# Hybrid encoder trunk on one core: places and order of the rotary queries and weight halves in the attention heads

## The chip, the core and the metric

The kernel runs on one core of one Trainium2 chip. Its engines work side by side, each through its own list of instructions in order: TensorE (PE, with its weight loads PEld) multiplies and transposes, VectorE (DVE), ScalarE (ACT) and GpSimd (POOL) work element by element, and SyncE (SP) starts the transfers from HBM to SBUF. Matmuls write to PSUM, from where DVE and ACT read.

The metric is the device time of one execution in microseconds (us). A change is judged by the median of several runs.

## The reference

The model has two layers over 256 tokens of width 2048, all in float32. Layer 0 mixes tokens with a convolution module, layer 1 with multi-head latent attention (16 heads), and each is followed by a squared-ReLU MLP of width 8192. The change is in the attention:

```python
down = h @ w_in
c_q, c_kv, k_pe = jnp.split(down, [Q_LORA_RANK, Q_LORA_RANK + KV_LORA_RANK], axis=-1)
q = (rms_norm(c_q, q_norm_g) @ w_q_up).reshape(B, S, N_HEADS, QK_NOPE_DIM + QK_ROPE_DIM)
q_nope, q_pe = jnp.split(q, [QK_NOPE_DIM], axis=-1)
q_pe = apply_rope(q_pe, cos[:, :, None, :], sin[:, :, None, :])
k_pe = apply_rope(k_pe, cos, sin)
kv = (rms_norm(c_kv, kv_norm_g) @ w_kv_up).reshape(B, S, N_HEADS, QK_NOPE_DIM + V_HEAD_DIM)
k_nope, v = jnp.split(kv, [QK_NOPE_DIM], axis=-1)
...
s = (jnp.einsum('bqhd,bkhd->bhqk', qn, k_nope)
     + jnp.einsum('bqhr,bkr->bhqk', qp, k_pe)).astype(jnp.float32) * scale
...
p = jax.nn.softmax(s, axis=-1).astype(v.dtype)
return jnp.einsum('bhqk,bkhd->bqhd', p, v)
```

Here `S` is 256, a head has 128 plain and 64 rotary query columns and 128 value columns, and a mask lets a token see only its own and earlier chunks of 64.

## The kernel before

**Numbers in two parts.** A float32 operand of a matmul is split into a high part (ACT copies it to a narrower type, `hi`) and a low part (DVE subtracts, `lo`); three matmuls make one product (`mm3`, L178). Weights come as units of 0.5 or 1 MB in a `raw` tile (three places) and are split in two halves (`split_half`, L148): one copy on ACT (L154) and one subtraction on DVE (L155) each, 128 x 1024 for most units, 128 x 512 for the rotary query units, into six places for halves.

**Pieces.** The attention part is one list in an order written out by hand (`manual_schedule`, L1147), and each engine gets its instructions in that order. The 16 heads form four groups of four (`HG`, `NG`). What a group needs ahead of its heads is cut into pieces:
- `qn_piece` (L1005): the plain queries of one head, transposed: 12 matmuls, then ACT writes `qTh` and DVE `qTl`;
- `qp_piece` (L1020): the rotary queries of four heads for one block `t` of 128 tokens: 12 matmuls, ACT copies PSUM to `qr` (L1030), POOL turns it in six steps (`rope`, L837 to L842) into `qp`, then ACT and POOL split `qp` into `qhl` (`qp_parts`, L1046);
- `kv_piece` (L978): keys of one head (`c` 0 or 1: `kTh`, `kTl`) or values of two heads for one block of tokens (`c` 2 or 3: DVE copies to `vv`), 12 matmuls each.

A group has four plain query pieces, two rotary ones and eight key and value pieces. While the heads of group g run, the pieces of group g+1 are put between their steps (during the last group, pieces of the output product).

**Steps of a head.** `scores(h)` (L1083): ten matmuls into one PSUM tile, then DVE takes the maxima (L1098, L1099) and ACT the exponentials (L1101). `weights(h)` (L1106): DVE scales (L1108, L1111). `weights_turn(h-1)` (L1113): three transposes on PE and a copy on ACT. `qp_turn` (L1050): four transposes of `qhl` for two heads of the next group, and two copies on ACT (`qpA` L1064, `qpB` L1065); the scores of these heads read `qpA` and `qpB` (L1095, L1096). `values(h-2)` (L1121): four matmuls, then a split on ACT and DVE.

All matmul results take turns in six PSUM tiles (`acc`, L133): a tile is written again when the engine that reads it is done, six tiles later.

**The queue of halves.** `start_unit(key, h)` (L907), called within a piece, puts half `h` of the unit two further on into `pending`; `prefetch(n)` (L914) takes up to `n` out: it issues the split, and after half 1 the load of the unit three further on, on SP's queue. Before the change the two halves are put in at the first and second piece of a unit.

**The wait list of the rotary split.** `qp_piece` appends its split to `later`; `piece` (L1038) runs what was in the list at its start behind the piece's own work, so the split comes at the end of the next piece.

**Order.** Ahead of the heads run all pieces of group 0, then `warm(AF.Exp)` (loads ACT's table), three plain query pieces of group 1 and both `qp_turn` of group 0 (L1224 to L1231). Then, for each head of group 0 to 2: scores, piece, `prefetch(1)`, piece, weights turn of the head before, from the third head of the group on a `qp_turn` for the next, values of the head two before, weights, `prefetch(1)`, and the remaining pieces, each with a `prefetch(1)`. The pieces left are spread evenly over the heads left (L1236): three each for heads 0 to 2 and two for head 3; 4, 4, 3, 3 in the two groups behind.

`scratch` is a 128 x 512 float32 tile in the pool `main`; ACT writes squares of no further use into it (`squares` L952, `prepare` L328), and ahead of the heads it holds the two mask rows (L934).

Of the kernel before, what the change touches and what calls it, by code (L numbers as in the profile page):

```python
# [10 lines left out]
F32 = mybir.dt.float32  # L11
# [7 lines left out]
P = 128  # L19
# [11 lines left out]
DR = 64  # L31
# [41 lines left out]
def trunk_kernel(  # L73
# [54 lines left out]
    def nm(s):  # L128
        uid[0] += 1
        return f"{s}_{uid[0]}"  # L130


    def acc_tile():  # L133
        return psum["acc"].tile([P, NB], F32, tag="acc", name=nm("acc"))
# [43 lines left out]
    def mm3(ps, sh, sl, mh, ml, start, stop):  # L178

        nc.tensor.matmul(ps, sh, mh, start=start, stop=False)  # L180
        nc.tensor.matmul(ps, sl, mh, start=False, stop=False)  # L181
        nc.tensor.matmul(ps, sh, ml, start=False, stop=stop)  # L182

    def hi_part(ps, hi, scale=1.0):

        nc.scalar.activation(hi, ps, AF.Copy, scale=scale)
# [121 lines left out]
    scratch = main.tile([P, NB], F32, name="scratch")  # L308
# [124 lines left out]
    with ExitStack() as cx:  # L433
# [172 lines left out]
        with tc.manual_schedule():  # L606
# [57 lines left out]
            for c in range(1, KC + 1):  # L664
                n = UC * c
# [22 lines left out]
                if 2 <= c < 2 + T * NNB:  # L688

                    t, i = divmod(c - 2, NNB)  # L690
# [136 lines left out]
    with ExitStack() as cx:  # L827
        at = cx.enter_context(tc.tile_pool(name="at", bufs=1, reuse_waits="tile"))
        at2 = cx.enter_context(tc.tile_pool(name="at2", bufs=2, reuse_waits="tile"))

        def rope(dst, src, t, nh, eng):

            a, b = src[:, :, 0:HR], src[:, :, HR:DR]
            cb = cos[:, t : t + 1, :].broadcast_to([P, nh, HR])
            sb = sin[:, t : t + 1, :].broadcast_to([P, nh, HR])
            m = [at2.tile([P, 4, HR], F32, tag=f"m{i}", name=nm("m"), bufs=1)[:, :nh, :] for i in range(4)]
            eng.tensor_tensor(m[0], a, cb, op=ALU.mult)  # L837
            eng.tensor_tensor(m[1], b, sb, op=ALU.mult)
            eng.tensor_tensor(m[2], b, cb, op=ALU.mult)
            eng.tensor_tensor(m[3], a, sb, op=ALU.mult)  # L840
            eng.tensor_tensor(dst[:, :, 0:HR], m[0], m[1], op=ALU.subtract)
            eng.tensor_tensor(dst[:, :, HR:DR], m[2], m[3], op=ALU.add)  # L842

        HG = 4
# [42 lines left out]
        def u_load(n):  # L887
            if n < len(units):
                srcs, shape = units[n]
                raw = raws[n] = wpool.tile(shape, F32, tag="raw", name=nm("raw"), bufs=3)  # L890
                for i, src in enumerate(srcs):
                    dst = raw if len(srcs) == 1 else raw[:, i : i + 1, :]
                    if len(src.shape) == 4:
                        dst = dst.rearrange("p j (h n) -> p j h n", h=src.shape[2])
                    nc.sync.dma_start(dst, src)

        def u_split(n, h):
            if n < len(units):
                parts[n, h] = split_half(raws[n], h, nc.vector)

        def w_at(key, j):
            n = pieces[key]
            half = units[n][1][1] // 2
            hi, lo = parts[n, j // half]
            return hi[:, j % half, :], lo[:, j % half, :]

        def start_unit(key, h):  # L907

            n = pieces[key]
            pending.append((n + LOOK, h))  # L910
# [3 lines left out]
        def prefetch(n=9):  # L914
            while pending and n > 0:
                n -= 1
                u, h = pending.pop(0)
                u_split(u, h)
                if h == 1:
                    u_load(u + 3)  # L920
# [50 lines left out]
        def parts_tile(tag):  # L971
            return [gp[0].tile([P, HG, S], F32R, tag=tag + c, name=nm(tag + c)) for c in "hl"]

        def in_parts(o, parts, i):
            hi_part(o, parts[0][:, i, :])
            lo_part(o, parts[0][:, i, :], parts[1][:, i, :])

        def kv_piece(g, i, c):  # L978

            key = ("kvu", g, i)  # L980
            if i == 0 and c == 0:
                kTs[g] = parts_tile("kT")
                vvs[g] = gp[0].tile([P, T, HG * DV], F32, tag="vv", name=nm("vv"))
            if c < 2:
                start_unit(key, c)
            po = acc_tile()
            if c < 2:
                o = po[:, :S]
                ns = slice(c * (DN + DV), c * (DN + DV) + DN)
                for j in range(NJ):  # L990
                    wh, wl = w_at(key, j)
                    nc.tensor.matmul(o, wh[:, ns], kvh[:, j, :], start=j == 0, stop=False)
                    nc.tensor.matmul(o, wh[:, ns], kvl[:, j, :], start=False, stop=False)
                    nc.tensor.matmul(o, wl[:, ns], kvh[:, j, :], start=False, stop=j == NJ - 1)
                in_parts(o, kTs[g], 2 * i + c)
            else:
                t = c - 2
                ts = slice(t * P, (t + 1) * P)
                o = po[:, : 2 * DV].rearrange("p (h n) -> p h n", h=2)
                for j in range(NJ):  # L1000
                    wh, wl = (a.rearrange("p (h n) -> p h n", h=2)[:, :, DN:] for a in w_at(key, j))
                    mm3(o, kvh[:, j, ts], kvl[:, j, ts], wh, wl, j == 0, j == NJ - 1)
                nc.vector.tensor_copy(vvs[g][:, t, 2 * i * DV : 2 * (i + 1) * DV], po[:, : 2 * DV])

        def qn_piece(g, i):  # L1005
            key = ("qn", g)
            if i == 0:
                qTs[g] = parts_tile("qT")
            if i < 2:
                start_unit(key, i)  # L1010
            o = acc_tile()[:, :S]
            ns = slice(i * DN, (i + 1) * DN)
            for j in range(NJ):
                wh, wl = w_at(key, j)
                nc.tensor.matmul(o, wh[:, ns], qh[:, j, :], start=j == 0, stop=False)
                nc.tensor.matmul(o, wh[:, ns], ql[:, j, :], start=False, stop=False)
                nc.tensor.matmul(o, wl[:, ns], qh[:, j, :], start=False, stop=j == NJ - 1)
            in_parts(o, qTs[g], i)

        def qp_piece(g, t):  # L1020
            key = ("qp", g)
            start_unit(key, t)
            o = acc_tile()[:, : HG * DR]
            ts = slice(t * P, (t + 1) * P)
            for j in range(NJ):
                wh, wl = w_at(key, j)
                mm3(o, qh[:, j, ts], ql[:, j, ts], wh, wl, j == 0, j == NJ - 1)

            qr = at2.tile([P, HG, DR], F32, tag="qr", name=nm("qr"), bufs=1)
            nc.scalar.activation(qr, o.rearrange("p (h n) -> p h n", h=HG), AF.Copy)  # L1030
            qp = at2.tile([P, HG, DR], F32, tag="qp", name=nm("qp"))
            rope(qp, qr, t, HG, nc.gpsimd)
            hl = qps[g, t] = at2.tile([P, HG, 2, DR], F32R, tag="qhl", name=nm("qhl"))
            later.append(lambda: qp_parts(qp, hl))

        later = []

        def piece(work):  # L1038

            due = list(later)  # L1040
            del later[:]
            work()
            for fn in due:
                fn()

        def qp_parts(qp, hl):  # L1046
            hi_part(qp, hl[:, :, 0, :])
            nc.gpsimd.tensor_tensor(hl[:, :, 1, :], qp, hl[:, :, 0, :].bitcast(F32), op=ALU.subtract)
# [18 lines left out]
        def kv_work(g):  # L1067
            return [lambda i=i, c=c: kv_piece(g, i, c) for i in range(HG // 2) for c in range(4)]
# [6 lines left out]
        def group_work(g):  # L1075
            kv = kv_work(g)
            return q_work(g) + kv
# [58 lines left out]
        def o_piece(k):  # L1136
            m, j = divmod(k, 2)
            if k == 0:
                ps_o.extend([[acc_tile() for _ in range(T)] for _ in range(2)])
            start_unit(("o", m), j)  # L1140
            wh, wl = w_at(("o", m), j)
            for b in range(2):
                bs = slice(b * NB, (b + 1) * NB)
                for t in range(T):
                    mm3(ps_o[b][t], oh_kt(k, t), ol_kt(k, t), wh[:, bs], wl[:, bs], k == 0, k == H - 1)

        with tc.manual_schedule():  # L1147
# [63 lines left out]
            work = kv_work(0)  # L1211
# [12 lines left out]
            work = group_work(1)  # L1224
            warm(AF.Exp)
            for w in work[:3]:
                prefetch(1)
                piece(w)
            for m in range(2):
                qp_turn(0, m)  # L1230
            work = work[3:]  # L1231
            for g in range(NG):
                for i in range(HG):
                    h = g * HG + i

                    n = -(-len(work) // (HG - i))  # L1236
                    todo, work = work[:n], work[n:]
# [17 lines left out]
                if g + 2 < NG:  # L1255
                    work = group_work(g + 2)
                elif g + 2 == NG:
                    work = [lambda k=k: o_piece(k) for k in range(H - HG)]
# [90 lines left out]
```

## Time and profile before

| what | us |
|---|---|
| median of three runs | 2022.86 (2021.18 to 2023.08) |
| profiled execution | 2022.87 |
| its span, first to last instruction | 2020.7 |
| TensorE busy | 1993.2 (99%) |
| VectorE busy | 1217.8 (60%) |
| ScalarE busy | 966.2 (48%) |
| GpSimd busy | 205.1 (10%) |

The attention pieces and heads run from about 1089 to 1260 us of the span. A row of the view in order of time gives the start, the duration, engine, line, operation and tiles, how many are merged, and in brackets how long the engine had been idle before it and what ended that. Matmuls are pipelined: the time between two starts is shorter than the duration of one, and is what counts. A row of the stretches gives start and end, length, the busy time of PE, PEld, DVE, ACT and POOL with the number of instructions, the clock granted to TensorE (1.00 is full), the share of the transfer engines and GB/s. A row of the waits gives the waiting engine with tile and line, what it waited for, the sum in us, how often, and the longest.

### The profile page before, as it was taken

To read this page: it belongs to the slowest core of one execution; us is meant where nothing else is said; L and a number is where in the kernel's file an instruction comes from. 1 tells how busy PE (TensorE), PEld (TensorE's weight loads), DVE (VectorE), ACT (ScalarE), POOL (GpSimd) and SP (SyncE) were. 2 spreads that over 40 slices of the span, in tenths; PEclk is the share of its full clock that TensorE was granted. 3 is DMA by queue.
4 is the path that set the end of the run, shared out by engine and by line. 5 is a ranking of instruction groups with operands and counts; after the bars stand their busy time and mean duration, and the time that the engine had idled before them with its cause. 6 is when DMAs were issued, how large, how long until landed. Compare 5 with 4: busy or idle time off the path is not lost. (4 is left out here: it accounts for less than half of the span.)

```text
span 2020.7 us, 27994 instructions
## 1 busy us (share of the span) xinstructions
PE 1993.2 (99%) x11144; PEld 1747.0 (86%) x11144; DVE 1217.8 (60%) x1806; ACT 966.2 (48%) x1372; POOL 205.1 (10%) x156
## 2 busy tenths in 40 slices
PE   7999999999999999999999999999999999999998
PEld 7999888888888888888889898888888888888886
DVE  6999866665544465555446665665654445565553
ACT  5444565544433354444445665554543334454443
POOL 5887300000000000000001310000000000000000
PEclk9999999999999999999999999999999999999999
DMA  7555355665555666555555445566655566655552
GB/s 237 168 167 167 126 189 186 190 189 192 199 189 190 193 192 192 191 187 189 187 165 159 121 144 174 187 197 192 194 189 189 197 197 188 188 187 190 199 195 104
DMA packets 243266, 367.58 MB, mean 182 GB/s; under 512 B 15416, under 2 KB 89792, under 8 KB 242880
## 3 DMA queue, kind: packets, MB, share of 16 engines
q1 hardware_dynamic: 242400, 364.68, 56.2%
q8 instruction: 87, 1.43, 0.3%
q10 hardware_dynamic: 736, 1.12, 0.2%
q14 instruction: 43, 0.35, 0.0%
HBM read 363.68 MB, written 2.10 MB: 181 GB/s over the span
## 5 line engine op out<-in xcount | busy, mean ns | idle before, releaser
L155 DVE TENSOR_TENSOR lo<-raw,hi 128x1024 fp32r<-128x1024 f32 (+2 forms) x629 | 760.1, 1211 | 693.0 <-ACT hi L154 681.1
L154 ACT ACTIVATE hi<-raw 128x1024 fp32r<-128x1024 f32 (+1 forms) x696 | 723.4, 1046 | 787.3 <-PE acc L181 451.3
L399 PE MATMUL acc<-xt,hi 128*128 128x512 f32 x2048 | 710.6, 390 | 0.0
L400 PE MATMUL acc<-xt,lo 128*128 128x256 f32 x2048 | 578.1, 282 | 0.0
L399 PEld LDWEIGHTS acc<-xt,hi 128*128 128x128 f32 x2048 | 384.4, 188 | 79.7
L180 PE MATMUL acc<-hi,gh 128*128 128x512 f32 x1024 | 398.8, 389 | 0.0
L182 PE MATMUL acc<-lo,gh 128*128 128x512 f32 x1024 | 398.6, 389 | 0.0
L181 PE MATMUL acc<-hi,gl 128*128 128x512 f32 x1024 | 398.6, 389 | 0.0
L400 PEld LDWEIGHTS acc<-xt,lo 128*128 128x128 f32 x2048 | 387.8, 189 | 0.1
L180 PEld LDWEIGHTS acc<-hi,gh 128*128 128x128 f32 x1024 | 192.3, 188 | 40.0
L181 PEld LDWEIGHTS acc<-hi,gl 128*128 128x128 f32 x1024 | 192.3, 188 | 39.7
L182 PEld LDWEIGHTS acc<-lo,gh 128*128 128x128 f32 x1024 | 192.3, 188 | 39.5
L552 DVE SCALAR_TENSOR_TENSOR sum<-ub,w_dw,sum 128x256 f32<-128x256 f32 x404 | 168.7, 484 | 2.7 <-ACT sum L521 0.7
L155 POOL TENSOR_TENSOR lo<-raw,hi 128x1024 fp32r<-128x1024 f32 x67 | 159.2, 2399 | 56.6 <-ACT hi L154 56.6
L485 PE MATMUL acc<-xt,hi 128*128 128x256 f32 x512 | 147.2, 287 | 0.0
L486 PE MATMUL acc<-xt,hi 128*128 128x256 f32 x512 | 143.2, 280 | 1.0 <-DVE xt L193 1.0
L487 PE MATMUL acc<-xt,lo 128*128 128x256 f32 x512 | 143.0, 279 | 0.0
L486 PEld LDWEIGHTS acc<-xt,hi 128*128 128x128 f32 x512 | 96.4, 188 | 1.6 <-DVE xt L193 1.2
L485 PEld LDWEIGHTS acc<-xt,hi 128*128 128x128 f32 x512 | 96.4, 188 | 0.4
L487 PEld LDWEIGHTS acc<-xt,lo 128*128 128x128 f32 x512 | 96.3, 188 | 0.0
L923 POOL MEMSET pad_kv<- 128x8 f32 x1 | 0.1, 104 | 772.6 <-PE acc L182 772.6
L407 ACT ACTIVATE v<-acc 128x256 f32<-128x256 f32 x128 | 46.4, 381 | 25.4 <-PE acc L400 25.4
(230 smaller groups left out, 1788.0 us busy)
## 6 DMA issues: line engine op xcount, KB each, us to landing
raw<-in_mlp_w SPq DMA_DIRECT2D x256, 1024.0 KB, 5.1
raw<-in_conv_w_pw SPq DMA_DIRECT2D x64, 512.0 KB, 5.0
raw<-in_conv_w_pw SPq DMA_DIRECT2D x16, 1024.0 KB, 5.0
raw<-in_mla_w_o SPq DMA_DIRECT2D x16, 1024.0 KB, 5.3
raw<-in_mla_w_kv_up SPq DMA_DIRECT2D x8, 1024.0 KB, 5.3
raw<-in_mla_w_in SPq DMA_DIRECT2D x8, 576.0 KB, 3.7
raw<-in_mla_w_in SPq DMA_DIRECT2D x4, 1024.0 KB, 6.6
raw<-in_mla_w_q_up SPq DMA_DIRECT2D x16, 256.0 KB, 3.5
```

Of the source, the lines that this page charges most:

```text
L154: nc.scalar.activation(hi, raw[:, js, :], AF.Copy)
L155: eng.tensor_tensor(lo, raw[:, js, :], hi.bitcast(F32), op=ALU.subtract)
L180: nc.tensor.matmul(ps, sh, mh, start=start, stop=False)
L181: nc.tensor.matmul(ps, sl, mh, start=False, stop=False)
L182: nc.tensor.matmul(ps, sh, ml, start=False, stop=stop)
L399: nc.tensor.matmul(ps[b], wh[:, bs], xhl(k), start=k == 0, stop=False)
L400: nc.tensor.matmul(ps[b][:, :S], wl[:, bs], xh(k), start=False, stop=k == KC - 1)
L407: nc.scalar.activation(v[:, b, :], o[:, S:], AF.Copy)
L485: nc.tensor.matmul(o, wh[:, bs], xh(k), start=k == 0, stop=False)
L486: nc.tensor.matmul(o, wh[:, bs], xl(k), start=False, stop=False)
L487: nc.tensor.matmul(o, wl[:, bs], xh(k), start=False, stop=k == KC - 1)
L552: nc.vector.scalar_tensor_tensor(out=out, in0=ubs[c][:, w : w + S], scalar=tap(c, w), in1=pcs[c], op0=ALU.mult, op1=ALU.add)
```

## The change

The instructions stay the same in kind and number. Four things are different.

- The copy `qr` of the rotary queries had one place of its own; now the two blocks `t` go to the two halves of `scratch`.
- The split of a rotary query block comes at the end of the third piece behind its own (the fourth in group 0), where it was the next one.
- A unit's two halves are put into the queue at its first and third piece (key and value units: `c` 0 and 2; plain query units: `i` 0 and 2), where it was the first and second. The load of a further unit moves with the second half.
- Two more pieces of group 1 (its last plain query piece and first rotary one) run between the first `qp_turn` calls and `scores(0)`. Nine pieces are left for heads 0 to 3: three for head 0 and two for each of the others.

```diff
-            if c < 2:
-                start_unit(key, c)
+            if c % 2 == 0:
+                start_unit(key, c // 2)
...
-            if i < 2:
-                start_unit(key, i)
+            if i % 2 == 0:
+                start_unit(key, i // 2)
...
-            qr = at2.tile([P, HG, DR], F32, tag="qr", name=nm("qr"), bufs=1)
+            qr = scratch[:, t * HG * DR : (t + 1) * HG * DR].rearrange("p (h n) -> p h n", h=HG)
             nc.scalar.activation(qr, o.rearrange("p (h n) -> p h n", h=HG), AF.Copy)
             qp = at2.tile([P, HG, DR], F32, tag="qp", name=nm("qp"))
             rope(qp, qr, t, HG, nc.gpsimd)
             hl = qps[g, t] = at2.tile([P, HG, 2, DR], F32R, tag="qhl", name=nm("qhl"))
-            later.append(lambda: qp_parts(qp, hl))
+            later.append([4 if g == 0 else 3, lambda: qp_parts(qp, hl)])
...
             due = list(later)
-            del later[:]
             work()
-            for fn in due:
-                fn()
+            for e in due:
+                e[0] -= 1
+                if e[0] == 0:
+                    later.remove(e)
+                    e[1]()
...
             for m in range(2):
                 qp_turn(0, m)
-            work = work[3:]
+            for w in work[3:5]:
+                piece(w)
+                prefetch(1)
+            work = work[5:]
```

## The prediction

> **What bounds the kernel now.** I read the busy shares first, then the waits of the tensor engine, then the stretches of the attention heads, and last the four engines in order of time there.
>
> ```profile
> PE 1993.2 (99%) x11144; PEld 1747.0 (86%) x11144; DVE 1217.8 (60%) x1806; ACT 966.2 (48%) x1372; POOL 205.1 (10%) x156
> ```
>
> The tensor engine (PE) is busy for 99% of the span, so only its own waits can be won back. In the heads it has these (engine, line, what it waited for, us in total, times, longest):
>
> ```profile
> PE acc L180 <- ACT pr L1101: 2.3, 2, 1.1
> PE acc L1095 <- ACT qpA L1064: 2.2, 1, 2.2
> PE acc L992 <- DVE qTl L191: 0.9, 1, 0.9
> ...
> PE tr L1117 <- DVE pr L1111: 0.3, 2, 0.2
> ```
>
> None of them is a wait for a transfer. They sum to 5.7 us, but a wait costs more than its idle time. Busy time by stretches (us, then PE, PEld, DVE, ACT, POOL; then the granted clock):
>
> ```profile
> 1120.00:1121.00 1.00, 1.00 (x7) 1.00 (x6) 0.19 (x2) 0.74 (x4) 0.00 (x0) 0.50 0.96 267
> 1121.00:1122.00 1.00, 1.00 (x6) 1.00 (x6) 0.00 (x0) 0.35 (x3) 0.00 (x0) 0.50 1.06 312
> ...
> 1115.17:1143.38 28.21, 25.66 (x201) 24.95 (x199) 16.83 (x38) 16.65 (x40) 8.46 (x14) 0.94 0.44 129
> 1143.38:1176.43 33.05, 30.71 (x247) 29.31 (x246) 21.03 (x52) 20.22 (x55) 8.46 (x14) 1.00 0.38 113
> 1176.43:1207.27 30.84, 29.70 (x247) 29.12 (x246) 21.13 (x48) 18.34 (x47) 8.47 (x14) 1.00 0.41 137
> ```
>
> The last three stretches are heads 0 to 3 (from the first scores on), 4 to 7 and 8 to 11, each with the projections of the next group. The first two rows show the clock at half speed soon after the 2.2 us wait; over its stretch it is 0.94, so 0.06 x 28.21 = 1.7 us are lost while PE looks busy.
>
> What each stretch would take without waits comes from the spacing of the matmuls (start, duration, engine, line; in brackets the idle time before):
>
> ```profile
> 1104.58 0.28 PE L1015 MATMUL acc<-qh,hi 128*128 128x256 f32 x1
> ...
> 1114.38 1.04 PE L1055 MATMUL tr<-ident,qhl 128*128 128x128 f32 x8
> 1115.17 0.30 PE L180 MATMUL acc<-kTh,qTh 128*128 128x128 f32 x1
> ...
> 1117.93 0.33 PE L1095 MATMUL acc<-kpA,qpA 128*128 128x128 f32 x1 [2.23 <-ACT qpA L1064]
> ...
> 1180.42 0.49 PE L1117 MATMUL tr<-ident,pr 128*128 128x128 f32 x3
> 1180.75 0.60 PE L1126 MATMUL acc<-pT,vv 128*128 128x256 f32 x2
> 1181.32 0.37 PE L1015 MATMUL acc<-qh,hi 128*128 128x256 f32 x1
> ...
> 1184.24 0.22 PE L180 MATMUL acc<-kTh,qTh 128*128 128x128 f32 x1
> 1185.39 0.28 PE L1015 MATMUL acc<-qh,hi 128*128 128x256 f32 x1
> ...
> 1193.54 0.33 PE L180 MATMUL acc<-kTh,qTh 128*128 128x128 f32 x1 [1.14 <-ACT pr L1101]
> ```
>
> From 1104.58 to 1114.38 run seven pieces of twelve matmuls: 1.40 us each. Two pairs of first turns (eight transposes) take 1115.17 - 1114.38 = 0.79, so 0.40 a pair. A head's weights turn is 0.33, its values 0.57, its scores 1.15; two pieces behind values take 2.92, so values cost 0.12 more there. Heads 4 to 7 need 14 x 1.40 + 4 x 1.15 + 4 x (0.33 + 0.57 + 0.12) + 2 x 0.40 = 29.1; heads 8 to 11 the same; heads 0 to 3 (11 pieces, 3 weights turns, 2 values) 15.4 + 4.6 + 1.0 + 1.4 + 0.8 = 23.2. Lost: 28.21 - 23.2 = 5.0, 33.05 - 29.1 = 3.95, 30.84 - 29.1 = 1.75. Sum 10.7 us: all that can be won.
>
> **What makes PE wait.** ScalarE (ACT) takes its work in program order, and waits for GpSimd's rotary work (POOL) in the middle of it:
>
> ```profile
> 1106.56 0.38 ACT L1030 ACTIVATE qr<-acc 128x256 f32<-128x256 f32 x1 [1.86 <-POOL m L840]
> ...
> 1110.90 0.42 ACT L186 ACTIVATE qhl<-qp 128x256 fp32r<-128x256 f32 x1 [1.86 <-POOL qp L842]
> ...
> 1112.53 0.65 ACT L186 ACTIVATE qTh<-acc 128x256 fp32r<-128x256 f32 x2
> ...
> 1114.86 1.05 ACT L154 ACTIVATE hi<-raw 128x1024 fp32r<-128x1024 f32 x1
> 1115.81 0.37 ACT L186 ACTIVATE qTh<-acc 128x256 fp32r<-128x256 f32 x1
> 1116.07 1.05 ACT L154 ACTIVATE hi<-raw 128x1024 fp32r<-128x1024 f32 x1
> ...
> 1117.28 0.60 ACT L1064 ACTIVATE qpA<-tr 128x512 fp32r<-128x512 f32 x1
> ...
> 1183.51 0.38 ACT L1030 ACTIVATE qr<-acc 128x256 f32<-128x256 f32 x1 [1.85 <-POOL m L840]
> 1184.35 0.42 ACT L186 ACTIVATE qhl<-qp 128x256 fp32r<-128x256 f32 x1 [0.45 <-POOL qp L842]
> ```
>
> The 1.86 is the second rotary copy (`qr` has one place) waiting until POOL has read the first. From starts: a weight half costs ACT 1115.81 - 1114.86 = 0.95, a 256-wide copy 1116.07 - 1115.81 = 0.26 and a qpA copy lasts 0.60. VectorE (DVE) then runs late:
>
> ```profile
> 1113.67 0.74 DVE L191 TENSOR_TENSOR qTl<-acc,qTh 128x256 fp32r<-128x256 f32 x2
> ...
> 1147.12 0.15 DVE L1108 RECIPROCAL zs<-zs 128x2 f32<-128x2 f32 x1
> ...
> 1147.78 0.62 DVE L1098 TENSOR_REDUCE mx<-acc 128x1 f32<-128x128 f32 x2
> ...
> 1186.90 1.76 DVE L155 TENSOR_TENSOR lo<-raw,hi 128x1024 fp32r<-128x1024 f32 x1
> ...
> 1188.92 1.42 DVE L155 TENSOR_TENSOR lo<-raw,hi 128x1024 fp32r<-128x1024 f32 x1
> ...
> 1190.60 1.21 DVE L155 TENSOR_TENSOR lo<-raw,hi 128x1024 fp32r<-128x1024 f32 x1
> 1191.73 0.61 DVE L1098 TENSOR_REDUCE mx<-acc 128x1 f32<-128x128 f32 x2
> ```
>
> Three weight halves stand ahead of head 9's maxima. Its scores were issued by 1185.39; the maxima start at 1191.73, the exponentials follow (1.8 from there until PE goes on), and the scores of head 10, six PSUM tiles later, wait for that tile: the 1.14 of 1193.54. Heads 4 to 7 lose more because PE comes early to them.
>
> **The change, part by part.** It removes and adds no instruction and no transfer; places and order change.
>
> Rotary copies in two halves of `scratch`: the 1.86 of ACT goes, four times. The scratch is written by ACT itself before, and POOL has read the last group's copy long before the next: no new wait.
>
> Their split later: the hi copy of `qhl` moves behind two more pieces (three for group 0). The 0.45 goes in the steady groups: the copy then stands behind some 4 us of other ACT work, while POOL needs six steps of 0.46 a rotary. In group 0 POOL runs beside two weight halves of DVE:
>
> ```profile
> 1105.09 1.44 POOL L840 TENSOR_TENSOR m<-qr,sin 128x128 f32<-128x128 f32 x1
> 1106.49 0.46 POOL L841 TENSOR_TENSOR qp<-m,m 128x128 f32<-128x128 f32 x1
> ```
>
> One step of 0.46 becomes 1.44 beside a half. The second rotary's end was 1110.9; with the halves now closer together I bound it by 1110.9 and 1112.0 (one more such step). ACT gets to that copy at 1110.7 and waits 0.2 to 1.3. Behind it stand the table load and the first halves of group 1; qpA, which also needs the turns of 1115.17, then ends at 1115.6 to 1116.1.
>
> Two pieces between first turns and scores: PE gets 2 x 1.40 = 2.8 of work there, so scores(0) wants qpA at 1115.2 + 2.8 = 1118.0. Cover 1.9 to 2.4; the 2.23 goes, and with it the half clock. Without that cover PE would ask near 1115.7 (1117.93 - 2.23) and wait up to 0.4.
>
> On that half clock, the row first: it followed 2.23 us without a matmul. [...]
>
> Weight halves at every other piece: the second half comes one piece (1.4 us) later for the key/value and query units, and so does the 1 MB load behind it on SP's queue. Their time to landing (KB each, median us):
>
> ```profile
> raw<-in_mla_w_kv_up SPq DMA_DIRECT2D x8, 1024.0 KB, 5.3
> ```
>
> A load is issued three units ahead of its use and is wanted 9 us or more after its trigger in the steady groups: nothing. The closest is the query rotary unit of group 1, which ACT comes to sooner now; if its load were late, ACT would wait, but PE doesn't ask for it before 1116.6. In steady groups the halves ahead of the second head's maxima become two: 1.2 to 1.4 less. One half moves instead ahead of the first head's maxima: 0 to 1.2 more there.
>
> Steady groups summed: the second head's exponentials come 1.85 + 0.45 + 1.2 to 1.4 earlier, less 0 to 1.2: 2.3 to 3.7. Heads 8 to 11 need 1.75 (their whole loss; PE then wants the tile that much sooner): margin 0.5 to 2. Heads 4 to 7 need 3.95. There head 4's exponentials start 5.3 after its scores,
>
> ```profile
> 1148.69 0.37 ACT L1101 ACTIVATE pr<-acc,mx 128x128 f32<-128x128 f32 x1 [1.94 <-DVE mx L1099]
> ```
>
> and 4.7 in my walk below: 0.6 more, so 2.9 to 4.3 against 3.95. No half moves ahead of head 4's maxima that wasn't there, so I take the upper end, 0.3 over; at the lower end 1.0 stays.
>
> New waits: heads 1 to 3 now have two pieces instead of three between scores, so less PE work covers the way scores, maxima, exponentials, weights, turn. In my walk, PE starts scores(1) at 1123.4 and wants weights(1) at 1131.6 (two scores, four pieces, one turn). DVE, with 0.7 for maxima, 1147.78 - 1147.12 = 0.66 for weights and 1.2 to 1.4 a half, has maxima(0) done at 1121.7 to 1122.3, the third half at 1125.3 to 1125.9 (its ACT copy stands behind exponentials and the second rotary copy), maxima(1) at 1128.4 to 1129.0, weights(1) at 1131.8 to 1132.4: a wait of 0.2 to 0.8. The same walk gives 0 to 0.5 at head 2's turn, none at head 3's. I take 0.8 for both. For small waits like the 0.3 at the weights turns I leave 0.3 a group, and 0.3 for the thin margin of heads 4 to 7: 1.2.
>
> **The sum.** The profiled execution took 2022.87 us (span 2020.7), which is 0.01 from the median of the three runs. 2022.87 - 10.7 + 0.8 + 1.2 = 2014.2. Its own bounds: 2012.2 with no wait left, 2016.3 with 1.3 of new ones, 1.0 in heads 4 to 7 and 0.6 a group of small ones. Behind the heads PE is the limit and no transfer is waited for, so the gain is kept.
>
> **The rivals.** [...]
>
> *The two copies don't come apart*: the halves of `scratch` are guarded as one tile, and ACT still waits its 1.86. Against it: ACT writes two slices of `qTh` back to back at 1112.53, and DVE reads the first at 1113.67, so slices are guarded one by one. Then steady groups save only 0.45 + 1.2 of the 2.3 to 3.7, and keep about 1.1 each: 2014.2 + 2.2 = 2016.4.
>
> *Only the first group gains*: POOL stretches the two remaining halves to 1.76, and the extra half ahead of the first head's maxima counts whole, so that the margins go and the old waits come back. It decides from 2 us of DVE delay a group more than I count. Gain 5.0 - 0.8 - 0.3 = 3.9: 2019.0.
>
> *Slower: the thin heads.* With two pieces a head the turns of heads 1 and 2 wait, and from 2.2 us on each pulls the clock down as the old one did. Price of one: the 5.0 of heads 0 to 3. Two of them with nothing won in later groups: 2022.87 - 5.0 + 10.0 = 2027.9. It decides if weights(1) comes 2.2 us late, where I count 0.2 to 0.8.
>
> **How the numbers follow.** Forecast 0.63, half clock stays 0.08, copies together 0.11, first group alone 0.11, thin heads 0.07. The predicted time is 2014.2. The first three together are 0.82 and reach from 2012.2 to 2016.4; with half a microsecond to a microsecond for the spread of runs (2021.18 to 2023.08) the range is 2011.7 to 2017.3. What a measurement can tell from no change is about 0.2%, 4.0 us: faster 0.82 (the first three), same 0.11 (2019.0), slower 0.07.
>
> **What would show it.** Right: no idle of PE ahead of L1095 in the first scores and a clock of 1.00 through the heads; the second rotary copy right behind the first half's hi copy with no wait for POOL; two halves ahead of the maxima of heads 5 and 9; heads 4 to 7 and 8 to 11 in about 29.4 each. A wait of L1117 for weights at heads 1 and 2 below 1 us. Wrong: `qr` still waiting for L840; a fall of the clock at heads 2 to 3; a wait of L180 for the exponentials in heads 6 and 10.

## The result and the profile after

| | before | after |
|---|---|---|
| median (range; five runs each) | 2022.93 (2021.18 to 2023.13) | 2014.3 (2014.11 to 2014.59) |
| profiled execution | 2022.87 | 2014.30 |
| its span | 2020.7 | 2012.4 |

The ratio is 0.9959, with a 95% interval of 0.9944 to 0.9973: 8.6 us faster. The wide interval comes from the kernel before, whose executions fall on levels about 1.5 us apart; the last section returns to them.

The changed lines shift the numbering by two or three: the turns of weights are now L1119, the first rotary scores L1097, the copies of `qpA` and `qpB` L1066 and L1067, the maxima L1100 and L1101, the exponentials L1103, the scaling of weights L1113. The tile `qr` is called `scratch`.

The busy shares after:

```profile
PE 1989.3 (99%) x11144; PEld 1743.9 (87%) x11144; DVE 1217.5 (61%) x1806; ACT 966.0 (48%) x1372; POOL 209.3 (10%) x156
```

PE has the same 11144 instructions and is busy 3.9 us less; POOL is busy 4.2 us more, with the same 156 instructions. The waits of the tensor engine in the heads, of which there were four kinds, are now one:

```profile
PE tr L1119 <- DVE pr L1113: 1.2, 2, 1.0
```

The stretches (first turns to scores of head 4, then to head 8, then to head 12), first before, then after:

```profile
1114.38:1143.38 29.00, 26.45 (x208) 25.75 (x206) 17.04 (x39) 17.43 (x43) 8.46 (x14) 0.94 0.44 131
```

```profile
1114.55:1140.50 25.95, 24.75 (x208) 24.09 (x206) 17.72 (x40) 15.73 (x42) 9.35 (x14) 1.00 0.43 131
1140.50:1169.74 29.24, 29.24 (x247) 29.04 (x246) 20.00 (x48) 19.14 (x52) 9.58 (x14) 1.00 0.43 127
1169.74:1198.95 29.21, 29.21 (x247) 29.00 (x246) 20.79 (x47) 18.49 (x48) 9.57 (x14) 1.00 0.45 144
```

The first stretch is taken from the turns on here, since two pieces now lie between them and the scores; from there the ideal of the prediction is 23.2 + 0.8 = 24.0. The gains are 29.00 - 25.95 = 3.05, 33.05 - 29.24 = 3.81 and 30.84 - 29.21 = 1.63, in all 8.49. The turns start 0.17 later than before (1114.55 against 1114.38), which leaves 8.32, and the span is 8.3 shorter: nothing is won or lost elsewhere. In the second and third stretch PE is busy for the whole length, at full clock. Of the 3.9 us of busy time that went, 1.70 are in heads 0 to 3 (26.45 - 24.75), where the half clock is gone, and 1.96 in the two behind (30.71 - 29.24 and 29.70 - 29.21), where the waits are gone.

PE at the places that waited before, and where it waits now:

```profile
1118.54 0.27 PE L1097 MATMUL acc<-kpA,qpA 128*128 128x128 f32 x1
...
1133.02 0.70 PE L1119 MATMUL tr<-ident,pr 128*128 128x128 f32 x3 [0.96 <-DVE pr L1113]
...
1139.04 0.61 PE L1119 MATMUL tr<-ident,pr 128*128 128x128 f32 x3 [0.24 <-DVE pr L1113]
```

The first rotary scores start with no idle time; before they waited 2.23. The turns of heads 1 and 2 wait 0.96 and 0.24. ScalarE in group 0, and then in group 1's heads:

```profile
1103.59 0.38 ACT L1030 ACTIVATE scratch<-acc 128x256 f32<-128x256 f32 x1 [2.25 <-PE acc L182]
1103.87 1.05 ACT L154 ACTIVATE hi<-raw 128x1024 fp32r<-128x1024 f32 x1
1104.94 0.39 ACT L1030 ACTIVATE scratch<-acc 128x256 f32<-128x256 f32 x1
...
1112.10 0.42 ACT L186 ACTIVATE qhl<-qp 128x256 fp32r<-128x256 f32 x1 [1.16 <-POOL qp L842]
...
1115.68 0.61 ACT L1066 ACTIVATE qpA<-tr 128x512 fp32r<-128x512 f32 x1
...
1150.73 0.47 ACT L186 ACTIVATE qhl<-qp 128x256 fp32r<-128x256 f32 x1
```

The second rotary copy (1104.94) comes right behind a weight half, without the 1.86 of before. One wait for POOL is left, the 1.16 of group 0's second `qhl` copy, and it holds up nothing on PE: `qpA` is done at 1115.68 + 0.61 = 1116.29, 2.25 ahead of 1118.54. DVE in head 5:

```profile
1150.28 1.48 DVE L155 TENSOR_TENSOR lo<-raw,hi 128x1024 fp32r<-128x1024 f32 x1
...
1152.02 1.21 DVE L155 TENSOR_TENSOR lo<-raw,hi 128x1024 fp32r<-128x1024 f32 x1
...
1153.48 0.60 DVE L1100 TENSOR_REDUCE mx<-acc 128x1 f32<-128x128 f32 x2
```

Two halves stand ahead of its maxima, as the change means them to.

### The profile page after: what moved, and what is told of

The parts are those of the page before. It is cut to its first block, busy times and chain, and to the rows that moved or that the text cites. A ratio compares the mean times of both kernels' runs of the same rounds, so it can differ in the third digit from the quotient of the medians.

```text
span 2012.4 us, 28002 instructions
## 1 busy us (share of the span) xinstructions
PE 1989.3 (99%) x11144; PEld 1743.9 (87%) x11144; DVE 1217.5 (61%) x1806; ACT 966.0 (48%) x1372; POOL 209.3 (10%) x156
## 4 chain that ended last, share of the span: by engine, by line
PE 96%; DVE 2%; ACT 1%; DMA 0%; issue 0%; POOL 0%; SPq 0%; ACTq 0%; DVEq 0%
PE acc L399 23%; PE acc L182 16%; PE acc L180 16%; PE acc L181 16%; PE acc L400 12%; PE acc L486 3%; PE acc L485 3%; PE acc L487 3%; PE sum L518 1%; PE tr L237 1%; DMA xs<-in_x 0%; PE acc L1128 0%; PE acc L992 0%; PE acc L994 0%; PE acc L993 0%
```

## The experiments

Each kernel is the changed one or the one before with the edit shown. The table gives the median (range), its ratio to the kernel before run beside it with the 95% interval, and the three stretches of one profiled execution in us. The kernel before ran beside them in three rounds, with medians of 2022.82, 2022.98 and 2022.97, so a difference of 0.2 us between kernels says nothing.

| kernel | median | ratio | to head 4 | 4 to 8 | 8 to 12 |
|---|---|---|---|---|---|
| before | 2022.93 | 1 | 29.00 | 33.05 | 30.84 |
| after | 2014.3 | 0.9959 | 25.95 | 29.24 | 29.21 |
| after, later split undone | 2020.13 (2019.95–2020.37) | 0.9987 [0.9978, 0.9997] | 27.07 | 31.78 | 31.43 |
| after, two places undone | 2016.89 (2016.65–2017.19) | 0.9974 [0.9965, 0.9984] | 25.89 | 30.74 | 30.30 |
| after, halves undone | 2014.17 (2013.96–2014.31) | 0.9961 [0.9946, 0.9975] | 25.27 | 29.97 | 29.21 |
| after, two pieces undone | 2013.44 (2013.30–2013.61) | 0.9955 [0.994, 0.997] | 25.12 | 29.29 | 29.17 |
| before + places and later split | 2016.04 (2014.66–2016.17) | 0.9963 [0.995, 0.9976] | 27.67 | 29.29 | 29.17 |
| before + two pieces | 2019.53 (2019.31–2019.89) | 0.9985 [0.9975, 0.9994] | 26.22 | 32.82 | 30.84 |
| before + halves | 2020.8 (2020.48–2021.73) | 0.999 [0.998, 1.0] | 28.09 | 31.99 | 31.29 |
| before + wait filled | 2021.38 (2021.14–2021.56) | 0.9994 [0.9985, 1.0004] | 27.45 | 33.05 | 30.85 |
| after, a half behind the weights | 2013.98 (2013.93–2014.13) | 0.9958 [0.9943, 0.9973] | 24.25 | 30.56 | 29.20 |
| two pieces undone, split later still | 2012.93 (2012.81–2013.33) | 0.9955 [0.9941, 0.997] | 24.65 | 29.29 | 29.17 |

### The later split undone

```diff
-            later.append([4 if g == 0 else 3, lambda: qp_parts(qp, hl)])
+            later.append([1, lambda: qp_parts(qp, hl)])
```

> The changed kernel with the rotary split at the end of the next piece again. Theory: two places alone bring nothing, since the wait moves to the split: ACT reaches it at once and waits some 2.5 us for POOL to end the first rotary and again for the second, 1 to 3 us later than now in all, so PE waits 1 to 3 us in heads 6 and 10 each, and up to 1 more in heads 0 to 3: 2016.5 to 2021. Rival (the places matter, the delay does not): 2014.0 to 2015.0.

It takes 5.8 us more than the change (2020.13 - 2014.3). ScalarE's waits for POOL, and the row of group 1's second copy:

```profile
ACT qhl L186 <- POOL qp L842: 11.5, 7, 2.4
```

```profile
1151.30 0.42 ACT L186 ACTIVATE qhl<-qp 128x256 fp32r<-128x256 f32 x1 [2.42 <-POOL qp L842]
```

Before, the second rotary copy waited 1.85 and the split behind it 0.45, 2.3 together. With two places and the split where it was, the split waits the whole 2.42. So the two places by themselves only move the wait; POOL is busy as long as before in the two later stretches (8.45 and 8.47, before 8.46 and 8.47). And PE waits again, 2.0 in all at five turns of weights, and for `qTl` in heads 5 and 9, where before it did so in head 5 alone:

```profile
1155.99 0.39 PE L992 MATMUL acc<-kvh,hi 128*128 128x256 f32 x1 [0.91 <-DVE qTl L191]
...
1187.41 0.38 PE L992 MATMUL acc<-kvh,hi 128*128 128x256 f32 x1 [0.91 <-DVE qTl L191]
```

### The two places undone

```diff
-            qr = scratch[:, t * HG * DR : (t + 1) * HG * DR].rearrange("p (h n) -> p h n", h=HG)
+            qr = at2.tile([P, HG, DR], F32, tag="qr", name=nm("qr"), bufs=1)
```

> The changed kernel with one place for the rotary copy again. Theory: the second copy waits 1.8 us for POOL's fourth step in each steady group, everything behind it on ACT and DVE comes that much later, and since head 5's exponentials ended only 0.7 us ahead of PE's need, PE waits about 1.2 us in heads 6 and 10: 2016.2 to 2017.0. Rival (the later split alone gives the slack): 2014.0 to 2014.8.

2.6 us more than the change. The wait sits at the copy once more:

```profile
ACT qr L1030 <- POOL m L840: 5.6, 3, 1.9
```

```profile
1149.18 0.38 ACT L1030 ACTIVATE qr<-acc 128x256 f32<-128x256 f32 x1 [1.86 <-POOL m L840]
```

Heads 4 to 7 lose 30.74 - 29.24 = 1.50 and heads 8 to 11 lose 30.30 - 29.21 = 1.09. So each of the two edits needs the other: with one place ACT stops at the copy, with the early split at the split.

### Places and later split alone

The kernel before with these two edits of the change, and neither the halves nor the two pieces.

> The kernel before with two places and the later split alone (halves adjacent, no pieces moved). Theory: these two carry the gain. Against the run without the two pieces, one more half stands ahead of qpA, so the wait in scores(0) is about 1.4 us in place of 0.46, and heads 4 to 7 take about 0.7 us more: 2014.0 to 2015.2 if a wait of 1.4 us leaves the clock alone, 2015.7 to 2017 if it pulls it down. Rival (all four are needed): 2017 or more.

```profile
1141.98:1171.27 29.29, 29.29 (x247) 29.09 (x246) 19.25 (x47) 19.54 (x54) 10.60 (x14) 1.00 0.43 126
1171.27:1200.44 29.17, 29.17 (x246) 28.96 (x245) 21.09 (x49) 18.89 (x49) 10.61 (x14) 1.00 0.44 145
```

The whole gain of heads 4 to 11 is here. The first stretch is 27.67, because its wait stays in part, and the clock falls behind it:

```profile
1117.11 0.33 PE L1097 MATMUL acc<-kpA,qpA 128*128 128x128 f32 x1 [1.48 <-ACT qpA L1066]
```

```profile
1120.00:1121.00 1.00, 1.00 (x7) 1.00 (x7) 0.00 (x0) 0.59 (x3) 0.00 (x0) 0.50 1.12 335
```

The five executions lie at 2014.66 and 2014.76, and at 2016.04 to 2016.17; the profiled one, with the fall, belongs to the upper three; the two others were probably without the fall.

### The halves undone

```diff
-            if c % 2 == 0:
-                start_unit(key, c // 2)
+            if c < 2:
+                start_unit(key, c)
...
-            if i % 2 == 0:
-                start_unit(key, i // 2)
+            if i < 2:
+                start_unit(key, i)
```

> The changed kernel with the halves of a unit at its first and second piece again. Theory: three halves stand ahead of the maxima of heads 5 and 9 again (1.2 us), which is more than the 0.7 us of slack left there, so waits of about 0.5 us in heads 6 and 10, and about as much won back in heads 1 and 2, where a half gets out of the way of head 0's maxima: 2013.8 to 2015.3. Rival (this edit carries the gain of the steady groups): 2016.5 or more.

The time is that of the change (2014.17 against 2014.3, and the ranges overlap). It only moves within the kernel: 0.68 less in heads 0 to 3 (25.95 - 25.27), 0.73 more in heads 4 to 7 (29.97 - 29.24), where three halves now stand ahead of head 5's maxima and PE waits for its exponentials. Heads 8 to 11, where I expected such a wait too, stay at 29.21:

```profile
1149.54 1.48 DVE L155 TENSOR_TENSOR lo<-raw,hi 128x1024 fp32r<-128x1024 f32 x1
1151.28 1.21 DVE L155 TENSOR_TENSOR lo<-raw,hi 128x1024 fp32r<-128x1024 f32 x1
1152.75 1.21 DVE L155 TENSOR_TENSOR lo<-raw,hi 128x1024 fp32r<-128x1024 f32 x1
1153.88 0.61 DVE L1100 TENSOR_REDUCE mx<-acc 128x1 f32<-128x128 f32 x2
```

```profile
1155.80 0.33 PE L180 MATMUL acc<-kTh,qTh 128*128 128x128 f32 x1 [0.29 <-ACT pr L1103]
```

### The halves alone

The kernel before with the halves at every other piece.

> The kernel before with the halves at every other piece alone. Theory: one half of 0.95 us leaves ACT's way ahead of qpA, so scores(0) waits about 1.3 us in place of 2.23; heads 4 to 11 gain about 1 us each group, since two halves in place of three stand ahead of the maxima. If the clock falls only behind the longer wait, 2017.5 to 2019; if it falls behind 1.3 us as well, 2019.2 to 2020.7. Rival (ACT's waits for POOL hide it all): 2022 or more.

2.1 us faster than the kernel before by the medians, with an interval that reaches 1, and 0.1 above the range that I gave. Heads 4 to 7 gain 33.05 - 31.99 = 1.06, but heads 8 to 11 lose 31.29 - 30.84 = 0.45, where I had expected about 1 us won in both. There one half more stands ahead of head 8's maxima, and its exponentials start 4.42 after the start of the stretch (1179.18 - 1174.76) where it was 3.10 (1179.53 - 1176.43). PE no longer waits 1.14 for head 9's exponentials, but 0.91 for a `qTl` while head 9 runs. The first rotary scores wait 1.29, and the clock falls behind it in the profiled execution. That one, 2021.56, is among the slowest three of ten; the other seven lie at 2020.48 to 2020.96:

```profile
1117.29 0.33 PE L1095 MATMUL acc<-kpA,qpA 128*128 128x128 f32 x1 [1.29 <-ACT qpA L1064]
```

```profile
1120.00:1121.00 1.00, 1.00 (x7) 1.00 (x7) 0.00 (x0) 0.53 (x3) 0.00 (x0) 0.50 0.00 0
```

### The wait filled

```diff
                 qp_turn(0, m)
+            keep_warm(ident, 18)
             work = work[3:]
```

Eighteen more transposes of the identity, whose output nothing reads, behind the first turns of the kernel before: PE stays at work, but gets nothing done.

> The kernel before with 18 transposes of no use (18 x 0.11 = 2.0 us) on PE between the first turns and scores(0), where it waited 2.23 us. Theory (the wait pulls the clock down): PE is busy there, clock 1.00 from 1119 to 1123, 1.7 us less at the same place, 2020.8 to 2021.6. Rival (the half clock has another cause): clock still at half, 2022.5 to 2023.3.

```profile
1115.15 2.13 PE L220 MATMUL acc<-ident 128*128 128x128 f32 x18
1117.83 0.33 PE L1095 MATMUL acc<-kpA,qpA 128*128 128x128 f32 x1 [0.27 <-ACT qpA L1064]
```

```profile
1120.00:1121.00 1.00, 1.00 (x11) 1.00 (x10) 0.12 (x1) 0.84 (x5) 0.00 (x0) 1.00 0.94 280
1121.00:1122.00 1.00, 1.00 (x11) 1.00 (x10) 0.59 (x3) 0.34 (x2) 0.00 (x0) 1.00 1.11 302
```

The scores come as late as before, yet the clock stays at 1.00 and the stretch is 29.00 - 27.45 = 1.55 shorter; the two behind it are unchanged. All ten executions lie at 2021.14 to 2021.56, the lowest of the levels on which the kernel before falls, and their median is 1.5 below its own (2022.93 - 2021.38; the interval of the ratio reaches past 1, since it takes in all these levels). The half clock follows from the wait, and is worth about 1.5 us.

### The two pieces alone

The kernel before with the two pieces between turns and scores.

> The kernel before with the two pieces alone. Theory: the 2.23 wait and the half clock go (4.2 us), but ACT still waits for POOL and heads 1 and 2 are thin, so new waits at the weights turns of 1 to 3 us in all; heads 4 to 11 keep their 5.7 us. 2019.5 to 2022. Rival (the two pieces carry the whole gain): 2014 to 2016. Rival (thin heads pull the clock down): a turn waits over 2 us, half clock behind it, 2024 or more.

3.4 us faster (2022.93 - 2019.53): the 2.23 and the half clock go, 2.78 in the first stretch, in which a new wait of 0.58 at head 1's turn is already counted. The turns wait 1.1 in all, where they waited 0.3: less than the 1 to 3 more that I expected. The later stretches are nearly as before, with the waits that the other edits remove:

```profile
1133.19 0.70 PE L1117 MATMUL tr<-ident,pr 128*128 128x128 f32 x3 [0.58 <-DVE pr L1111]
...
1155.28 0.39 PE L992 MATMUL acc<-kvh,hi 128*128 128x256 f32 x1 [0.91 <-DVE qTl L191]
...
1159.76 0.33 PE L180 MATMUL acc<-kTh,qTh 128*128 128x128 f32 x1 [1.13 <-ACT pr L1101]
```

### The two pieces undone

```diff
-            for w in work[3:5]:
-                piece(w)
-                prefetch(1)
-            work = work[5:]
+            work = work[3:]
```

> The changed kernel without the two pieces between first turns and scores (heads 0 to 3 get 3, 3, 3, 2 pieces again). Theory: ACT alone is now early enough, its qpA copy ended at 1116.3 where scores(0) would ask at 1115.7, so a wait of about 0.5 and no fall of the clock; the thin heads' waits of 0.96 and 0.24 go too. 2013.2 to 2014.8, clock 1.00 throughout. Rival (the two pieces are what removes the wait and the half clock): the wait is 2 us or more, the clock falls again, 2017.5 to 2019.

0.9 us faster than the change. With the other edits the wait is only 0.46, the clock stays at 1.00 behind it in the profiled execution, and the turns of heads 1 and 2, which have their third piece back, don't wait:

```profile
1116.31 0.33 PE L1097 MATMUL acc<-kpA,qpA 128*128 128x128 f32 x1 [0.46 <-ACT qpA L1066]
```

```profile
1114.53:1139.65 25.12, 24.53 (x207) 24.14 (x206) 17.93 (x40) 16.18 (x43) 9.68 (x14) 1.00 0.45 135
```

So in this combination the two pieces cost more than they cover.

### A half behind the weights

In the changed kernel, within the first group, the `prefetch` between a head's two pieces is left out for all heads but the first, so that halves wait until behind the weights:

```diff
                     piece(todo.pop(0))
-                    prefetch(1)
+                    if g > 0 or i == 0:
+                        prefetch(1)
                     piece(todo.pop(0))
```

> The changed kernel where heads 1 to 3 issue their waiting half behind the weights alone, not between the two pieces. Theory: weights(1) and weights(2) come about 1.2 us earlier, the waits of 0.96 and 0.24 at the turns go, and nothing new waits: 2012.6 to 2013.4. Rival (the half, now ahead of the next head's maxima, makes that head late by as much): 2014.0 to 2014.8.

The first stretch has no wait left and is 24.25, 1.70 less. But the halves that were put off come later, and heads 4 to 7 pay 30.56 - 29.24 = 1.32 for it, 0.47 of it as idle time of PE (30.56 - 30.09):

```profile
1114.50:1138.75 24.25, 24.25 (x207) 24.03 (x206) 17.23 (x38) 15.19 (x39) 9.34 (x14) 1.00 0.44 134
1138.75:1169.31 30.56, 30.09 (x248) 29.34 (x246) 20.75 (x51) 19.64 (x54) 9.56 (x14) 1.00 0.43 122
```

Its time is 0.3 below the change, not the 0.9 to 1.7 that I expected. The cause of the waits at the turns is shown (take the half away from them and they go); as an improvement it fails, since PE comes to heads 5 and 6 before their operands:

```profile
1155.03 0.33 PE L180 MATMUL acc<-kTh,qTh 128*128 128x128 f32 x1 [0.18 <-ACT pr L1103]
...
1158.15 0.39 PE L180 MATMUL acc<-hi,kvh 128*128 128x256 f32 x1 [0.29 <-DVE qTl L191]
```

### Two pieces undone, split later still

On top of the kernel without the two pieces, group 0's second rotary is split one piece later:

```diff
-            later.append([4 if g == 0 else 3, lambda: qp_parts(qp, hl)])
+            later.append([4 + t if g == 0 else 3, lambda: qp_parts(qp, hl)])
```

> The changed kernel without the two pieces, and group 0's second rotary split one piece later still, behind the table load. Theory: ACT loads its table in the 1.16 us in which it waited for POOL, qpA comes about 1 us earlier, and the last wait of 0.46 us goes: 2012.7 to 2013.2, no wait of PE left in the heads. Rival (POOL's half of the split now comes too late for the first turns): PE waits there, 2013.5 to 2014.5.

```profile
1111.14 1.28 ACT L214 ACT_TABLE_LOAD   x1
...
1112.81 0.41 ACT L186 ACTIVATE qhl<-qp 128x256 fp32r<-128x256 f32 x1
...
1115.37 0.60 ACT L1066 ACTIVATE qpA<-tr 128x512 fp32r<-128x512 f32 x1
```

The table load now lies in the time in which ACT waited for POOL, the copy of `qhl` finds its operand ready, and `qpA` is done at 1115.97, 0.32 earlier than in the changed kernel. I expected about 1 us; it is just enough, since PE asks for it at 1116.02. PE waits nowhere in the heads. 2012.93 is 1.4 below the change and the best of all kernels here; its slowest execution (2013.33) is faster than the change's fastest (2014.11).

## Why the prediction was right

**The mechanism.** Predicted 2014.2, measured 2014.3. Of its steps:

- *The two copies come apart*: right. No wait of L1030 for POOL, and the second copy right behind a weight half.
- *The later split takes the 0.45*: right, and it does more than its row says. Undone, ACT waits 2.42 and the time rises by 5.8; the 0.45 was small only because the 1.85 stood ahead of it. I counted them together, so the sum holds.
- *ACT waits 0.2 to 1.3 for group 0's second `qhl` copy*: 1.16. In the first rotary three steps of POOL instead of one ran beside DVE's halves (in the second, one of 0.91 in place of one of 1.44):

```profile
1105.31 1.45 POOL L840 TENSOR_TENSOR m<-scratch,sin 128x128 f32<-128x128 f32 x1
1106.73 1.44 POOL L841 TENSOR_TENSOR qp<-m,m 128x128 f32<-128x128 f32 x1
1108.13 0.97 POOL L842 TENSOR_TENSOR qp<-m,m 128x128 f32<-128x128 f32 x1
```

  POOL is done at 1112.07, at the late end of the 1110.9 to 1112.0 that I gave, and `qpA` ends at 1116.29 where I had 1115.6 to 1116.1 (0.17 of it is the later start). The cover of the two pieces, 2.25, lies in the predicted 1.9 to 2.4.
- *The half clock goes with the wait*: right, and shown by filling the wait: the clock is 1.00 then and the stretch 1.55 shorter, where I counted 1.7.
- *Without the two pieces, a wait of up to 0.4*: 0.46 in the run.
- *Two halves ahead of the second head's maxima*: right, as an order. It saves less than the 1.2 to 1.4 a group that I counted: undone beside the other edits it costs 0.73 in heads 4 to 7 and nothing in heads 8 to 11, and gives back 0.68 in heads 0 to 3.
- *A margin of 0.5 to 2 for heads 8 to 11, 0.3 for heads 4 to 7*: both stretches run without a wait. Head 5's exponentials end near 1155.4 and head 6's scores, which need their tile, start at 1156.10: 0.7 is over. Three halves instead of two use it up, as the 0.29 of that run shows.

**What was mis-sized.** Two terms, which cancel. *New waits of 0.8*, with 0.3 of small ones in heads 0 to 3, made 1.1; measured are 25.95 - 24.0 = 1.95. And *0.3 a group and 0.3 for the thin margin* made 0.9 for heads 4 to 11; measured are 29.24 + 29.21 - 58.2 = 0.25. So the sum is off by 0.85 one way and 0.65 the other, and that 2014.2 comes so near to 2014.3 is luck. The wait of head 1's turn was 0.96, above my 0.2 to 0.8, and DVE's rows tell why:

```profile
1127.33 1.22 DVE L155 TENSOR_TENSOR lo<-raw,hi 128x512 fp32r<-128x512 f32 x1
...
1131.42 0.81 DVE L155 TENSOR_TENSOR lo<-raw,hi 128x512 fp32r<-128x512 f32 x1 [1.48 <-ACT hi L154]
...
1132.67 0.55 DVE L1113 TENSOR_SCALAR pr<-pr,zs 128x128 f32<-128x128 f32 x2
```

My walk has the maxima of head 1 done at 1128.4 to 1129.0 and the weights 3.4 behind them. They were done at 1129.41, and the weights at 1133.22 (1132.67 + 0.55), 3.8 behind. The walk names no half between the two, but one of 0.81 stands there: its copy on ACT comes behind the exponentials, so DVE idles 1.48 for it and only then scales the weights. Put behind the weights, that half takes the wait with it, as the run shows. Of the 1.95, 1.20 is idle time, and 0.25 lies over the ideal even in the run without a wait (24.25). What the last 0.5 is, no run here shows.

**The rivals.** None came. The nearest to right was the one of the thin heads, in kind: the turns of heads 1 and 2 do wait, but 0.96 is under half of the 2.2 from which it decides, and the clock stays at 1.00. The price of *the two copies don't come apart* can be read off the run with one place: 2.6 more than the change, where I counted 2.2.

## What to carry to other kernels

When one engine waits twice in a row for the same slow helper, removing the first wait moves it to the second (here 1.85 and 0.45 became 2.42): give the copies their own places and put the use later, in one step, and judge neither alone. Work that covers a wait is taken from somewhere; once other edits have shortened the wait, look whether the cover still earns what it costs where it was taken, as the two pieces here did not (0.9 less without them). A stretch already free of waits shows no more gain, so an edit that is worth 2 us alone can be worth nothing beside others, as the halves here (2.1 alone).

## What was not expected of the hardware

**The half clock comes, by the times, in some executions and not in others, and behind shorter waits than the 2.2 us of the prediction.** In one profiled execution each, the clock fell to 0.50 behind idle times of PE of 2.23 us (the kernel before), 1.48 (places and later split alone) and 1.29 (halves alone), and did not behind 1.14 (the kernel before, twice), 1.13 (two pieces alone) and 0.96 (the changed kernel). And by the times it doesn't fall in every execution: the kernel with the 1.48 has two levels, 1.4 us apart, the lower at a mean granted clock of 0.999, the upper at 0.998. Beside the experiments the kernel before ran 52 times: 16 executions at 2021.24 to 2021.59 with a mean granted clock of 0.999, 29 at 2022.54 to 2023.33 with 0.998 (one 0.997), and 7 at 2024.14 to 2024.45 with 0.997. With the wait filled, all ten lie at 2021.14 to 2021.56, the lowest level. So of the 8.6 us won, about 1.5 are the half clock of a median execution of the kernel before, and by their times 16 of its 52 executions probably did not have it (the mean clock alone doesn't tell: two of the ten with the wait filled show 0.998 as well). What the third level adds was in no profile and stays open.

At a clock of 0.50, a slice of 1 us that shows a clock c was slow for 2 x (1 - c) us, so the kernel before was slow from 1119.40 to 1122.82, and again from 2017.12 on, behind PE's last work:

```profile
1119.00:1120.00 1.00, 1.00 (x9) 1.00 (x8) 0.60 (x2) 0.30 (x1) 0.00 (x0) 0.70 0.15 28
...
1122.00:1123.00 1.00, 1.00 (x7) 1.00 (x7) 0.73 (x4) 0.20 (x1) 0.00 (x0) 0.59 1.01 279
...
2017.00:2018.00 1.00, 0.00 (x0) 0.00 (x0) 0.00 (x0) 0.00 (x0) 0.00 (x0) 0.56 1.10 383
```

By the same sum the half clock lasts 3.42 us in the kernel before, 3.40 in the one with places and later split alone (clocks of 0.94, 0.50, 0.50, 0.50 and 0.86 in the slices from 1118 to 1123) and 3.42 in the one with the halves alone (0.98, 0.50, 0.50, 0.50 and 0.81): about the same behind the 2.23, the 1.48 and the 1.29. Why the clock falls in one execution and not in another, no run here shows.

**POOL beside DVE.** A step of 0.46 took 1.44 where it began within a subtraction of a weight half on DVE (before: the step at 1105.09, the subtraction from 1104.73 to 1106.21), and 0.97 where the subtraction was a shorter one (after: the step at 1108.13, the subtraction from 1108.10 to 1108.77). Three such steps in a row (1.45, 1.44 and 0.97) go with the two places and the later split: ACT no longer waits between its copies of two weight halves (1103.87 and 1105.22, before 1103.64 and 1107.72), so DVE's subtractions of them follow each other. In the three stretches together POOL is busy 30.10 us in the kernel with these two edits alone and 25.45 in the one with the halves alone, against 25.39 before and 28.49 after.
